# Attention: the combination's small sums on GpSimd over three turns, the last pair's quarters dealt to GpSimd and VectorE, the second branch stored in halves

## The chip, the cores and the metric

The kernel runs on one core of a Trainium2 chip. A core has five engines, each with its own queue of instructions that it works off in order: TensorE (PE in the profile) multiplies matrices and transposes, VectorE (DVE) and ScalarE (ACT) work on whole tiles, GpSimd (POOL) does elementwise work of the same kind, in this kernel on tiles outside TensorE's accumulators alone, and SyncE (SP) issues the transfers (DMAs) between the device's memory and the on-chip memory. Engines wait for one another by semaphores. The metric is device microseconds (us) of one launch, as the median of the runs.

## What is computed

One decoder layer over 2048 tokens of width 1024, all in float32. Half of the mixer's width is gated linear attention (GLA) in chunks, the other half is dilated attention with 8 heads of 64; then come an output projection, a squared-ReLU MLP and norms. The change lies in the dilated attention. Each head has three branches (window and dilation 128/1, 512/4 and 2048/16), and their results are weighted with a softmax over their log-sum-exps:

```python
def dilated_mixer(q, k, v, rel_bias):
    q = q * DSA_DH ** -0.5
    outs, lses = [], []
    for window, dilation in DSA_PATTERN:
        o, lse = dilated_branch(q, k, v, rel_bias, window, dilation)
        outs.append(o)
        lses.append(lse)
    w = jax.nn.softmax(jnp.stack(lses, axis=0), axis=0)
    return jnp.sum(w[..., None] * jnp.stack(outs, axis=0), axis=0)
```

The kernel doesn't form the log-sum-exps. For each token, head and branch it keeps the sum of the values weighted with exp(s - m), the sum of these weights (den) and nm = -m, the negated largest logit. The combination takes M, the smallest nm of the three branches, E = exp(M - nm), Z = the sum of E times den, and the weights E / Z.

## The kernel before

The kernel runs in stages, one after the other: the input projections, then the attention (the dilated attention with the GLA steps strewn into it), then the output projection and the MLP. In the projections and the MLP TensorE multiplies without a break; the change touches the attention alone, which lies between about 562 and 920 us.

**Units.** The dilated attention goes over four pairs of heads. A head has a sequence of 20 units: 4 for branch 2 (dilation 16), 8 for branch 1 (dilation 4), 8 for branch 0. So a pair has 40 units and the whole 160. In the last pair (pair 3) branches 2 and 1 of both heads come first and the branch-0 units of the two heads take turns of two at the end. The loop (L973) runs over units; in each turn three units at different stages are woven together instruction by instruction (`alternate`): the scores of the unit three ahead, the transposes of the present one and the values of the one two back.

- Scores: TensorE multiplies queries and keys into accumulator banks `ps_c` (L649 and L651); VectorE adds the bias and takes the minimum in one custom instruction (L661, tiles `pe` and `O`, where `O` takes nm), ScalarE forms the exponential (L662).
- Transposes: TensorE turns the weights into `ps_d` (L671); the copy into `pt` goes to ScalarE (L678) and to VectorE (L680) in turn.
- Values: TensorE multiplies `pt` with the values `v` into `ps_a` (L690); VectorE copies each finished group of four token blocks into `O` (L693).

So for every unit TensorE depends on VectorE at three places: L661 (its bank `ps_c` is free only when VectorE has read it), L680 and L693.

**The rest of the attention's work.** GLA steps follow one another at a fixed rate of 56 for each 100 units, using accumulator bank `ps_o` (L810 the decay, L823, L824, L867) and GpSimd for their elementwise work (L813, L816, L818, L860, L861, and the power in L98); VectorE adds the new state from `ps_o` (L870). GpSimd also packs each head's queries for branches 1 and 2 by casts (`pack_q`, L603, four pieces of 512 columns) and sets ones into the values' tile (L557). `load_v` (L554) fetches a pair's values; for branch 1 in four batches, one a unit.

**The combination.** The results of branches 2 and 1 stand in another order of tokens than those of branch 0. So when both heads of a branch are done, `store_branch` (L699) writes `O` out to `boD` and `combine_load` (L709) reads it back in token order into the tile `cmb`, half of the tokens (8 blocks of 128) at a time. `combine` (L717) then handles a half: 14 small sums on tiles of 128x16 (two minima L725 and L726, three subtractions L728, the denominators L730, L732, L733 twice, the reciprocal L734, three weights L736), and one Exp on ScalarE (L729). All 14 are on VectorE. Then come, for each four blocks, three 128x512 products (L742) and two additions (L744), on GpSimd. It is a generator that stops after the small sums and after each addition; `combine_at` (L927) gives it its turns. In pairs 0 to 2 the combination of a pair runs in the first units of the next pair, each half with 6 turns, the first three units after the pair's start. In pair 3 it runs in quarters of four blocks (sums of 128x8), at units that lie 8, 11, 14 and 18 after its branch-0 units begin, since the output projection's first tiles wait for it: TensorE's transposes of the first 8 token blocks take the last pair straight from `O` (L1051 and following). Quarter 12's products are on VectorE, those of the other three on GpSimd. The scratch `small` (128 x 96) is shared by both halves.

**What sets the order.** Each engine's queue is in the order that a tile scheduler makes of the program: it follows the program, and may put an instruction whose data it takes for ready ahead of others on the same engine. `keep_in_program_order` pins an instruction behind the one that was written before it on its engine. `issue_later` (L753) holds a transfer back for a number of units, `at_unit` plans a function for a unit.

Of the kernel before, what the change touches and what calls it, by code (L numbers as in the profile page):

```python
# [20 lines left out]
HT = NT // 2  # L21
# [19 lines left out]
def emit(tc, a, stop=99):  # L41
# [657 lines left out]
    def store_branch(pr, br, O):  # L699
        dst = boD[pr][br - 1]  # L700
        if br == 1:
            issue_later(3, dst.rearrange("(b p r) n -> p b (r n)", b=4, r=4),
                        O.rearrange("p (b r) n -> p b (r n)", b=4))
        else:
            issue_later(3, dst.rearrange("(p r) n -> p (r n)", r=16), O.rearrange("p r n -> p (r n)"))
# [11 lines left out]
    def combine(pr, t0, n, loaded, X):  # L717
# [3 lines left out]
        at = small[:, t0 // 4 % 2 * 48:] if n == 4 else small  # L721
# [3 lines left out]
        V.tensor_tensor(M, nm[0], nm[1], op=OP.min)  # L725
        V.tensor_tensor(M, M, nm[2], op=OP.min)  # L726
        for b in range(3):
            V.tensor_tensor(E[:, b], M, nm[b], op=OP.subtract)  # L728
        A.activation(E, E, AF.Exp)  # L729
        V.tensor_tensor(Z[:, 0], E[:, 0], den[0], op=OP.mult)  # L730
        for b in (1, 2):
            V.tensor_tensor(Z[:, 1], E[:, b], den[b], op=OP.mult)  # L732
            V.tensor_tensor(Z[:, 0], Z[:, 0], Z[:, 1], op=OP.add)  # L733
        V.reciprocal(Z[:, 1], Z[:, 0])  # L734
        for b in range(3):
            V.tensor_tensor(E[:, b], E[:, b], Z[:, 1], op=OP.mult)  # L736
# [28 lines left out]
    def gla_start():  # L765
# [16 lines left out]
        gst["sq"] = ub[:, 1800:1928]  # L782
        gst["gq"] = [view(uc[:, 256 * i:], (2, 128)) for i in range(2)]
# [128 lines left out]
    def after(b):  # L912
        pr, hh = divmod(b.h, 2)
        if hh and b.br:
            store_branch(pr, b.br, b.O)
        if hh and pr < 3:
            vs[pr + 1, b.br] = load_v(pr + 1, b.br, lambda n, *f: at_unit(clock[0] + AHEAD + 1 + n, *f))
# [9 lines left out]
    def combine_at(pr, t0, n, at, steps):  # L927
# [4 lines left out]
        def step():  # L932
            if (pr, t0) not in running:
                running[pr, t0] = combine(pr, t0, n, got[pr, t0 // 8], V if (pr, t0) == (3, 12) else G)
            next(running[pr, t0], None)
# [4 lines left out]
    for pr in range(4):  # L940
# [3 lines left out]
        for hh, br in seq:  # L944
# [7 lines left out]
            if br == 2 and first:  # L952
# [3 lines left out]
                if hh == 0:  # L956
                    for half in range(2):
                        combine_at(pr - 1, 8 * half, 8, first - 2 + 7 * half, [first + 3 + 7 * half + n for n in range(6)])
# [14 lines left out]
    for k in range(-AHEAD, NU + LAG):  # L973
# [18 lines left out]
        if 0 <= k - LAG:  # L992
            u = units[k - LAG]
            if u.ns[-1] == NT - 1:
                after(u.b)
    for _ in gla:
        pass
# [425 lines left out]
```

## Time and profile before

| | |
|---|---|
| median of 3 runs | 2352.82 us (2348.53 to 2355.7) |
| the profiled execution | 2354.68 us, with a span of 2352.9 us |
| TensorE busy, share of the span | 2292.8 us, 97% |
| VectorE | 1583.5 us, 67% |
| ScalarE | 1147.5 us, 49% |
| GpSimd | 467.3 us, 20% |
| mean granted TensorE clock | 0.992 |

A row of the timeline gives the start in us, the duration, the engine, the line, the operation, the tiles (out<-in), their shape, the number of instructions in the row, and in brackets the idle time of the engine ahead of it with what ended it. A row of the waits names the engine, the tile and line that waited, after the arrow what released it, then the sum of the waits in us, how many there were and the longest. A row of a group gives the number of instructions, the busy time and the mean duration in ns. A row of the windows gives a stretch, its length, each engine's busy time with its instructions, the granted TensorE clock (1.00 is full), the share of the DMA engines that were busy, and GB/s.

### The profile page before, as it was taken

How to read it: one execution, taken by the hardware profiler on the slowest of the kernel's cores; microseconds unless marked ns; L12 is line 12 of the kernel's file. 1: busy time of each engine (PE TensorE's matmuls, PEld its weight loads, DVE VectorE, ACT ScalarE, POOL GpSimd, SP SyncE). 2: the span in 40 equal slices, each digit the busy share in tenths (PEclk: the TensorE clock that was granted, in tenths of full speed). 3: DMA queues.
4: the chain of work that ended last, by engine and by line, in shares of the span. 5: the costliest groups of instructions: out<-in, count | busy, mean ns of one | idle time of the engine just before them, and what ended most of it. 6: DMA issues, size and time to landing. Idle time of an engine off the chain costs nothing.

```text
span 2352.9 us, 34987 instructions
## 1 busy us (share of the span) xinstructions
PE 2292.8 (97%) x12652; PEld 1978.6 (84%) x12652; DVE 1583.5 (67%) x2989; ACT 1147.5 (49%) x2200; POOL 467.3 (20%) x467
## 2 busy tenths in 40 slices
PE   6999999999999998999999999999999999999998
PEld 6978898689999988888888888888888888888887
DVE  7888778756677677345877779777764456446545
ACT  5665436435676664323655557555553223224323
POOL 0333324245486465100000000000000100001002
PEclk8999999999999999999999999999999999999999
DMA  4458754857676755567744447444476487457653
GB/s 151 138 166 246 223 176 121 256 166 235 193 231 212 251 166 195 188 215 255 252 163 148 148 148 273 148 150 155 155 262 238 170 283 246 145 179 250 207 169 108
DMA packets 341741, 457.59 MB, mean 194 GB/s; under 512 B 18053, under 2 KB 214166, under 8 KB 336192
## 3 DMA queue, kind: packets, MB, share of 16 engines
q1 hardware_dynamic: 336814, 446.71, 58.4%
q10 hardware_dynamic: 4754, 8.66, 1.0%
q8 instruction: 99, 1.62, 0.3%
q14 instruction: 74, 0.61, 0.1%
HBM read 292.99 MB, written 167.02 MB: 196 GB/s over the span
## 4 chain that ended last, share of the span: by engine, by line
PE 50%; DVE 1%; ACT 0%; issue 0%; POOL 0%; POOLq 0%
PE ps_c L67 6%; PE ps_c L68 6%; PE ps_c L66 6%; PE ps_a L68 4%; PE ps_a L67 4%; PE ps_a L66 4%; PE ps_d L66 4%; PE ps_d L68 4%; PE ps_d L67 4%; PE ps_o L68 2%; PE ps_o L67 2%; PE ps_o L66 2%; DVE hb L352 0%; ACT scr L1248 0%; DVE sumd L1254 0%; ACT hb L351 0%
## 5 line engine op out<-in xcount | busy, mean ns | idle before, releaser
L1250 POOL TENSOR_TENSOR suma<-suma,gs 128x512 f32<-128x512 f32 x16 | 23.3, 1474 | 1143.1 <-ACT scr L1248 1143.0
L352 DVE TENSOR_TENSOR ca<-ra,ca 128x1024 fp32r<-128x1024 f32 x112 | 137.6, 1230 | 162.1 <-ACT ca L351 161.9
L351 ACT ACTIVATE ca<-ra 128x1024 fp32r<-128x1024 f32 x112 | 118.0, 1053 | 219.5 <-PE ps_c L68 175.8
L351 ACT ACTIVATE w1comb<-w1raw 128x512 fp32r<-128x512 f32 x224 | 140.1, 627 | 156.3 <-PE ps_c L68 54.2
L690 PE MATMUL ps_a<-v,pt 128*128 128x65 f32 x1200 | 181.3, 254 | 8.8 <-DVE pt L680 7.5
L662 ACT ACTIVATE pe<-pe,O 128x256 f32<-128x256 f32 (+1 forms) x384 | 155.7, 454 | 67.1 <-DVE O L661 62.0
L352 DVE TENSOR_TENSOR w1comb<-w1raw,w1comb 128x512 fp32r<-128x512 f32 x224 | 153.9, 689 | 49.9 <-ACT w1comb L351 49.8
L690 PEld LDWEIGHTS ps_a<-v,pt 128*128 128x128 f32 x1200 | 176.9, 196 | 12.4 <-DVE pt L680 9.2
L671 PE MATMUL ps_d<-ident,pe 128*128 128x128 f32 x600 | 159.9, 280 | 0.0
L661 DVE CUSTOM_DVE_ANT_0 pe<-ps_c,nb 128x256 f32<-128x256 f32 (+1 forms) x384 | 126.0, 360 | 38.7 <-PE ps_d L671 17.0
L206 ACT ACTIVATE wcomb<-wraw 128x512 fp32r<-128x512 f32 (+2 forms) x126 | 96.9, 774 | 88.6 <-PE ps_o L67 19.3
L351 ACT ACTIVATE cb<-rb 128x1024 fp32r<-128x1024 f32 x56 | 59.4, 1061 | 164.5 <-PE ps_o L67 110.5
L67 PE MATMUL ps_c<-hb,w1comb 128*128 128x512 f32 x336 | 130.8, 389 | 0.7 <-DVE w1comb L352 0.7
L68 PE MATMUL ps_c<-hb,w1comb 128*128 128x512 f32 x336 | 130.7, 389 | 0.0
L66 PE MATMUL ps_c<-hb,w1comb 128*128 128x512 f32 x336 | 130.7, 389 | 0.0
L66 PE MATMUL ps_c<-cb,ca 128*128 128x512 f32 x336 | 130.7, 389 | 0.0
L67 PE MATMUL ps_c<-cb,ca 128*128 128x512 f32 x336 | 130.7, 389 | 0.0
L68 PE MATMUL ps_c<-cb,ca 128*128 128x512 f32 x336 | 130.7, 389 | 0.0
L208 DVE TENSOR_TENSOR wcomb<-wraw,wcomb 128x512 fp32r<-128x512 f32 (+2 forms) x84 | 96.3, 1150 | 36.0 <-ACT wcomb L206 35.6
L671 PEld LDWEIGHTS ps_d<-ident,pe 128*128 128x128 f32 x600 | 110.7, 189 | 0.3
L352 DVE TENSOR_TENSOR cb<-rb,cb 128x1024 fp32r<-128x1024 f32 x56 | 68.1, 1221 | 61.8 <-ACT cb L351 61.8
L1116 ACT ACTIVATE acc<-acc 128x512 f32<-128x512 f32 x128 | 79.7, 631 | 49.2 <-DVE acc L1136 34.9
(365 smaller groups left out, 7200.7 us busy)
## 6 DMA issues: line engine op xcount, KB each, us to landing
ra<-actD SPq DMA_DIRECT2D x56, 1024.0 KB, 7.2
actD<-acc SPq DMA_DIRECT2D x192, 256.0 KB, 2.4
rb<-w_ff SPq DMA_DIRECT2D x72, 512.0 KB, 4.6
w1raw<-w_ff SPq DMA_DIRECT2D x32, 1024.0 KB, 7.8
k<-kD SPq DMA_DIRECT2D x16, 1024.0 KB, 8.1
rb<-hTD SPq DMA_DIRECT2D x13, 1024.0 KB, 6.2
wraw<-w_in SPq DMA_DIRECT2D x48, 256.0 KB, 3.6
boD<-O SPq DMA_DIRECT2D x8, 1056.0 KB, 5.6
```

The source lines that it names most:

```text
L66: T.matmul(out, sh, mh, start=first, stop=False)
L67: T.matmul(out, sl, mh, start=False, stop=False)
L68: T.matmul(out, sh, ml, start=False, stop=last)
L206: A.activation(hi, src, AF.Copy, scale=sc)
L208: V.tensor_tensor(lo, src, hi.bitcast(F32), op=OP.subtract)
L351: A.activation(hi, src, AF.Copy)
L352: V.tensor_tensor(lo, src, hi.bitcast(F32), op=OP.subtract)
L661: V.tensor_tensor_reduce(p, s, bias, scale=1.0, scalar=BIG, op0=OP.add, op1=OP.min, accum_out=nm)
L662: A.activation(p, p, AF.Exp, bias=nm, scale=-1.0)
L671: T.transpose(pb[:, i * 128:i * 128 + 128], src, ident)
L690: T.matmul(self.b.opsum[:, n % 4], self.pt[:, i * 128:i * 128 + 128], self.b.v[:, blk, cols], start=first, stop=last)
L1116: A.activation(v, v, AF.Relu)
```

## The change

1. In pairs 0 to 2, 11 of a half's 14 small sums go to GpSimd: the three subtractions, the five operations for the denominators and the three weights. The two minima and the reciprocal stay on VectorE. The first minimum, the Exp and the reciprocal are pinned to the program's order. Two more stops in the generator spread the small sums over three turns (minima and subtractions; Exp and denominators; reciprocal and weights), and a half has 8 turns instead of 6, the first one unit later.
2. The second half has a scratch of its own (`gst["small"]`, in the tile that the profile calls `gla`).
3. In pair 3 the quarters that begin at block 0 and 8 are done by GpSimd, the small sums (without the minima and the reciprocal) and the products, and those that begin at block 4 and 12 by VectorE.
4. The store of branch 1 goes out in two halves, the first when the odd head's first eight blocks are done.
5. The four batches of the next pair's values lie two units apart, not one.

The lines move: of the changed kernel, L727 and L728 are the minima, L730 subtracts, L733 is the Exp, L734, L736 and L737 form the denominators, L740 is the reciprocal, L742 the weights, L748 the products and L750 the additions.

```diff
@@ -696,11 +696,12 @@
     class Branch:
         pass
 
-    def store_branch(pr, br, O):
+    def store_branch(pr, br, O, half=1):
         dst = boD[pr][br - 1]
         if br == 1:
-            issue_later(3, dst.rearrange("(b p r) n -> p b (r n)", b=4, r=4),
-                        O.rearrange("p (b r) n -> p b (r n)", b=4))
+            bs = slice(2 * half, 2 * half + 2)
+            issue_later(2 - half, dst.rearrange("(b p r) n -> p b (r n)", b=4, r=4)[:, bs],
+                        O.rearrange("p (b r) n -> p b (r n)", b=4)[:, bs])
         else:
             issue_later(3, dst.rearrange("(p r) n -> p (r n)", r=16), O.rearrange("p r n -> p (r n)"))
 
@@ -718,22 +719,27 @@
 
         ts = slice(t0, t0 + n)
         R = [outs[pr, 0][:, ts], *[r[:, t0 % 8:t0 % 8 + n] for r in loaded]]
-        at = small[:, t0 // 4 % 2 * 48:] if n == 4 else small
+        at = (small if t0 < 8 else gst["small"])[:, t0 // 4 % 2 * 48 if n == 4 else 0:]
         E, Z, M = view(at, (3, n, 2)), view(at[:, 6 * n:], (2, n, 2)), view(at[:, 10 * n:], (n, 2))
         nm = [r[:, :, 130:132] for r in R]
         den = [r[:, :, 0:130:129] for r in R]
-        V.tensor_tensor(M, nm[0], nm[1], op=OP.min)
+        W = X if pr == 3 else G
+        tc.keep_in_program_order(V.tensor_tensor(M, nm[0], nm[1], op=OP.min))
         V.tensor_tensor(M, M, nm[2], op=OP.min)
         for b in range(3):
-            V.tensor_tensor(E[:, b], M, nm[b], op=OP.subtract)
-        A.activation(E, E, AF.Exp)
-        V.tensor_tensor(Z[:, 0], E[:, 0], den[0], op=OP.mult)
+            W.tensor_tensor(E[:, b], M, nm[b], op=OP.subtract)
+        if pr < 3:
+            yield
+        tc.keep_in_program_order(A.activation(E, E, AF.Exp))
+        W.tensor_tensor(Z[:, 0], E[:, 0], den[0], op=OP.mult)
         for b in (1, 2):
-            V.tensor_tensor(Z[:, 1], E[:, b], den[b], op=OP.mult)
-            V.tensor_tensor(Z[:, 0], Z[:, 0], Z[:, 1], op=OP.add)
-        V.reciprocal(Z[:, 1], Z[:, 0])
+            W.tensor_tensor(Z[:, 1], E[:, b], den[b], op=OP.mult)
+            W.tensor_tensor(Z[:, 0], Z[:, 0], Z[:, 1], op=OP.add)
+        if pr < 3:
+            yield
+        tc.keep_in_program_order(V.reciprocal(Z[:, 1], Z[:, 0]))
         for b in range(3):
-            V.tensor_tensor(E[:, b], E[:, b], Z[:, 1], op=OP.mult)
+            W.tensor_tensor(E[:, b], E[:, b], Z[:, 1], op=OP.mult)
         yield
         for t in range(0, n, 4):
             rs = [r[:, t:t + 4, 1:129].rearrange("p t (h e) -> p t h e", h=2) for r in R]
@@ -780,6 +786,7 @@
         gst["kn"] = view(ub[:, 1032:], (2, 128))
         gst["g"] = [ub[:, 1288 + 256 * i:1544 + 256 * i] for i in range(2)]
         gst["sq"] = ub[:, 1800:1928]
+        gst["small"] = ub[:, 1928:2024]
         gst["gq"] = [view(uc[:, 256 * i:], (2, 128)) for i in range(2)]
         gst["gk"] = [view(uc[:, 512 + 256 * i:], (2, 128)) for i in range(2)]
         gst["gv"] = [uc[:, 1024 + 512 * i:1536 + 512 * i] for i in range(2)]
@@ -914,7 +921,7 @@
         if hh and b.br:
             store_branch(pr, b.br, b.O)
         if hh and pr < 3:
-            vs[pr + 1, b.br] = load_v(pr + 1, b.br, lambda n, *f: at_unit(clock[0] + AHEAD + 1 + n, *f))
+            vs[pr + 1, b.br] = load_v(pr + 1, b.br, lambda n, *f: at_unit(clock[0] + AHEAD + 1 + 2 * n, *f))
 
     units = []
     plan = {}
@@ -931,7 +938,7 @@
 
         def step():
             if (pr, t0) not in running:
-                running[pr, t0] = combine(pr, t0, n, got[pr, t0 // 8], V if (pr, t0) == (3, 12) else G)
+                running[pr, t0] = combine(pr, t0, n, got[pr, t0 // 8], V if pr == 3 and t0 % 8 else G)
             next(running[pr, t0], None)
 
         for k in steps:
@@ -955,7 +962,7 @@
                     at_unit(first - n, lambda p: next(p), pieces)
                 if hh == 0:
                     for half in range(2):
-                        combine_at(pr - 1, 8 * half, 8, first - 2 + 7 * half, [first + 3 + 7 * half + n for n in range(6)])
+                        combine_at(pr - 1, 8 * half, 8, first - 2 + 7 * half, [first + 4 + 7 * half + n for n in range(8)])
             if (pr, br) != (3, 0):
                 for n in range(0, NT, m):
                     units.append(Unit(b, range(n, n + m)))
@@ -993,6 +1000,8 @@
             u = units[k - LAG]
             if u.ns[-1] == NT - 1:
                 after(u.b)
+            elif u.ns[-1] == HT - 1 and u.b.h % 2 and u.b.br == 1:
+                store_branch(u.b.h // 2, 1, u.b.O, 0)
     for _ in gla:
         pass
     for k in range(NU + LAG + AHEAD, max(plan) + 1):
```

How the order of the engines' queues changes is shown at three places. The first is VectorE in the first units of pair 2, where the first half of pair 1 is combined (`O_6725`; `O_7541` is pair 2's). Before, nearly all the sums stand in a row between L661 steps:

```order
L725 TENSOR_TENSOR small<-O_6725,cmb 128x16
L661 ISA pe,O_7541<-ps_c,nb_5239 128x128
L661 ISA O_7541 128x1
L726 TENSOR_TENSOR small<-small,cmb 128x16
L661 ISA pe,O_7541<-ps_c,nb_5239 128x128
L661 ISA O_7541 128x1
L728 TENSOR_TENSOR small<-small,O_6725 128x16
L728 TENSOR_TENSOR small<-small,cmb 128x16 x2
L693 COPY O_6725<-ps_a 128x4x65
L680 COPY pt<-ps_d 128x512
L730 TENSOR_TENSOR small<-small,O_6725 128x16
L732 TENSOR_TENSOR small<-small,cmb 128x16
```

The same engine and combination in the changed kernel (`O_6721` is pair 1's, `O_7690` and `O_7539` are pair 2's), from the second minimum to the reciprocal:

```order
L728 TENSOR_TENSOR small<-small,cmb 128x16
L661 ISA pe,O_7690<-ps_c,nb_5266 128x256
L661 ISA O_7690 128x1
L693 COPY O_7539<-ps_a 128x4x65
L661 ISA pe,O_7690<-ps_c,nb_5266 128x256
L661 ISA O_7690 128x1
L680 COPY pt<-ps_d 128x256
L661 ISA pe,O_7690<-ps_c,nb_5266 128x256
L661 ISA O_7690 128x1
L693 COPY O_7539<-ps_a 128x4x65
L740 RECIPROCAL small<-small 128x16
L693 COPY O_7690<-ps_a 128x4x65
```

The subtractions, denominators and weights are gone from VectorE; three L661 steps, two copies of `O` and one of `pt` stand between the last minimum and the reciprocal.

The second place is GpSimd for the same half. Before, it has the products and additions, between the steps of the GLA:

```order
L97 TENSOR_SCALAR stats<-gla 128x4
L860 TENSOR_TENSOR gla<-gla 128x512
L98 TENSOR_TENSOR stats<-stats,mhalf 128x4
L742 TENSOR_TENSOR O_6725<-O_6725,small 128x4x128 x2
L742 TENSOR_TENSOR cmb<-cmb,small 128x4x128 x3
L861 TENSOR_TENSOR gla<-gla,stats 128x512
L742 TENSOR_TENSOR cmb<-cmb,small 128x4x128
L557 MEMSET v 128x16x2
L744 TENSOR_TENSOR O_6725<-O_6725,cmb 128x4x128 x2
```

In the changed kernel, on GpSimd (L820, L823 and L825 are the GLA's decay):

```order
L823 TENSOR_TENSOR gla<-gla 64x2x128 x2
L825 TENSOR_TENSOR gla<-gla 128x2
L820 TENSOR_TENSOR gla<-gla 128x256
L730 TENSOR_TENSOR small<-small,O_6721 128x16
L730 TENSOR_TENSOR small<-small,cmb 128x16 x2
L734 TENSOR_TENSOR small<-small,O_6721 128x16
L736 TENSOR_TENSOR small<-small,cmb 128x16
L737 TENSOR_TENSOR small<-small 128x16
L736 TENSOR_TENSOR small<-small,cmb 128x16
L737 TENSOR_TENSOR small<-small 128x16
L742 TENSOR_TENSOR small<-small 128x16 x3
L748 TENSOR_TENSOR O_6721<-O_6721,small 128x4x128 x2
```

The 11 sums stand in one block behind a decay of the GLA and ahead of the half's products.

The third place is VectorE in the last pair, at the end of the attention (`O_9505`, in the changed kernel `O_9507`, is pair 3's branch 0; L884 and L891 split the output projection's weights). Before:

```order
L734 RECIPROCAL small<-small 128x8
L884 TENSOR_TENSOR wo<-woraw,wo 128x1024
L732 TENSOR_TENSOR small<-small,cmb 128x8
L736 TENSOR_TENSOR small<-small 128x8 x3
L733 TENSOR_TENSOR small<-small 128x8
L734 RECIPROCAL small<-small 128x8
L736 TENSOR_TENSOR small<-small 128x8 x3
L693 COPY O_9505<-ps_a 128x4x65
L680 COPY pt<-ps_d 128x512
```

In the changed kernel, at the reciprocals of quarters 0 and 4:

```order
L740 RECIPROCAL small<-small 128x8 x2
L742 TENSOR_TENSOR small<-small 128x8
L891 TENSOR_TENSOR wo<-woraw,wo 128x1024
L742 TENSOR_TENSOR small<-small 128x8 x2
L748 TENSOR_TENSOR O_9507<-O_9507,small 128x4x128
L693 COPY O_9507<-ps_a 128x4x65
L680 COPY pt<-ps_d 128x512
L661 ISA pe,O_9507<-ps_c,nb_5301 128x256
L661 ISA O_9507 128x1
L748 TENSOR_TENSOR cmb<-cmb,small 128x4x128 x2
L891 TENSOR_TENSOR wo<-woraw,wo 128x1024
L680 COPY pt<-ps_d 128x512
```

Quarter 4's products now stand on VectorE between the copies and the L661 steps for which TensorE waits; one quarter's weights (L742) have left it.

## Prediction

> **What bounds the kernel now.** I read the page's first part, then a table of windows over the attention, then TensorE's list of waits there, and last the timeline around each long wait. The page's first part gives busy time by engine:
>
> ```profile
> span 2352.9 us, 34987 instructions
> PE 2292.8 (97%) x12652; PEld 1978.6 (84%) x12652; DVE 1583.5 (67%) x2989; ACT 1147.5 (49%) x2200; POOL 467.3 (20%) x467
> ```
>
> TensorE (PE) is busy for 97% of the span, so only its idle time and its clock can be won. The change touches the attention alone, so the next view is the windows of that stage: up to 630 us no combination runs, then come the stretches in which the combination of head pair 0, 1 and 2 runs, and the last 20 us before the output projection. After the length stand the busy times of PE, PE's loads, VectorE (DVE), ScalarE (ACT) and GpSimd (POOL), then the granted clock.
>
> ```profile
> 562.00:630.00 68.00, 68.00 (x628) 67.43 (x627) 47.17 (x198) 49.64 (x138) 35.87 (x49) 1.00 0.68 223
> 630.00:715.00 85.00, 82.47 (x732) 80.73 (x731) 62.88 (x275) 58.09 (x161) 58.85 (x67) 1.00 0.67 212
> 715.00:803.00 88.00, 85.92 (x752) 84.39 (x752) 62.89 (x275) 60.21 (x174) 61.00 (x71) 0.96 0.71 222
> 803.00:900.00 97.00, 89.35 (x759) 86.44 (x759) 73.24 (x300) 64.09 (x173) 50.74 (x57) 0.96 0.69 218
> 900.00:920.00 20.00, 15.17 (x117) 13.37 (x116) 17.73 (x52) 8.94 (x27) 17.75 (x17) 1.00 0.62 218
> ```
>
> Without a combination PE has no idle time at all; with one it loses 2.53, 2.08 and 7.65 us, and 4.83 us in the last stretch. Two stretches also have a clock under 1. So the combination is what stops PE. TensorE's list of waits in the attention says on whom:
>
> ```profile
> PE ps_a L690 <- DVE pt L680: 7.5, 8, 2.7
> PE ps_o L810 <- issue: 3.6, 2, 2.1
> PE ps_c L649 <- DVE O L661: 3.4, 3, 2.1
> PE ps_a L690 <- DVE O L693: 1.1, 1, 1.1
> PE ps_a L66 <- DVE O L693: 0.9, 1, 0.9
> PE ps_o L867 <- DVE gla L824: 0.3, 1, 0.3
> PE ps_a L690 <- ACT pt L678: 0.2, 1, 0.2
> ```
>
> Nearly all of it is VectorE, late with a copy or with the bias-and-minimum step (L661). GpSimd is in no row. The row "issue" names no one; the timeline shows what VectorE did then. Here are the long waits of PE with what VectorE and GpSimd did ahead of them (start, duration, instruction; in brackets the wait before it):
>
> ```profile
> 654.02 2.52 POOL L744 TENSOR_TENSOR O<-O,cmb 128x512 f32<-128x512 f32 x2
> 654.69 1.89 DVE L728 TENSOR_TENSOR small<-small,cmb 128x16 f32<-128x16 f32 x2
> 656.97 0.66 PE L690 MATMUL ps_a<-v,pt 128*128 128x65 f32 x4 [1.13 <-DVE O L693]
> ...
> 661.76 1.93 DVE L736 TENSOR_TENSOR small<-small 128x16 f32<-128x16 f32 x3
> 664.51 0.36 PE L649 MATMUL ps_c<-k,qs 128*128 128x256 f32 x1 [0.68 <-DVE O L661]
> ...
> 742.26 2.54 POOL L744 TENSOR_TENSOR O<-O,cmb 128x512 f32<-128x512 f32 x2
> 742.27 1.33 DVE L732 TENSOR_TENSOR small<-small,cmb 128x16 f32<-128x16 f32 x1
> 743.64 1.19 DVE L733 TENSOR_TENSOR small<-small 128x16 f32<-128x16 f32 x1
> 747.00 0.58 PE L649 MATMUL ps_c<-k,qs 128*128 128x256 f32 x1 [2.08 <-DVE O L661]
> ...
> 814.06 0.18 DVE L725 TENSOR_TENSOR small<-O,cmb 128x16 f32<-128x16 f32 x1 [4.60 <-DMA cmb<-boD]
> 815.10 0.57 PE L810 MATMUL ps_o<-gla 128*128 128x130 f32 x3 [1.56 <-issue]
> ...
> 833.45 1.25 DVE L728 TENSOR_TENSOR small<-small,cmb 128x16 f32<-128x16 f32 x1
> 834.62 3.86 POOL L603 CAST qp<-qs 128x512 fp32r<-128x512 f32 x4
> 835.44 0.39 PE L649 MATMUL ps_c<-k,qp 128*128 128x256 f32 x1 [0.62 <-DVE O L661]
> 836.55 0.90 DVE L732 TENSOR_TENSOR small<-small,cmb 128x16 f32<-128x16 f32 x1
> 838.32 0.90 PE L810 MATMUL ps_o<-gla 128*128 128x130 f32 x4 [2.08 <-issue]
> 839.88 0.69 PE L690 MATMUL ps_a<-v,pt 128*128 128x65 f32 x2 [0.66 <-DVE pt L680]
> ```
>
> A 128x16 sum is tiny, and a pair of them still holds VectorE for 1.9 us when GpSimd works on a product or a cast at the same time. At 814 VectorE stood for 4.60 us before a minimum whose data was still on its way.
>
> **Step 1: the waits that go.** In pairs 0 to 2, 11 of the 14 small sums of a half leave VectorE: the subtractions (L728), the weighted denominators (L730 to L733) and the weights (L736). Those are what stands ahead of the waits at 656.97, 664.51, 747.00, 835.44, 838.32 and 839.88. The two minima and the reciprocal stay, with a turn between each. The wait at 815.10 lies behind a minimum that a scheduler had pulled ahead of its data; after the change the minima are pinned to the program's place, a unit later (in the windows a pair of 40 units takes 88 us, so a unit is 2.2 us), and the store that feeds them goes out in two halves, the first one earlier. Removed: 1.13 + 0.68 + 2.08 + 1.56 + 0.62 + 2.08 + 0.66 = 8.8 us.
>
> **Step 2: the clock.** The two stretches under full clock come right behind the two waits of 2.08 us; a third row is the stretch behind the longest wait, in the last pair:
>
> ```profile
> 746.50:753.30 6.80, 6.30 (x27) 5.92 (x28) 4.82 (x20) 4.35 (x12) 6.63 (x8) 0.50 0.75 197
> 838.60:845.50 6.90, 6.24 (x34) 5.94 (x33) 4.31 (x24) 4.23 (x14) 4.92 (x6) 0.51 0.19 59
> 905.00:908.00 3.00, 2.99 (x27) 2.94 (x28) 3.00 (x7) 1.47 (x5) 3.00 (x3) 1.00 0.97 341
> ```
>
> The timeline has that longest wait:
>
> ```profile
> 902.35 1.67 DVE L736 TENSOR_TENSOR small<-small 128x8 f32<-128x8 f32 x3
> 905.01 0.44 PE L690 MATMUL ps_a<-v,pt 128*128 128x65 f32 x2 [2.68 <-DVE pt L680]
> ```
>
> At half clock PE needs twice the time, so 6.30/2 + 6.24/2 = 6.3 us are lost there. I take it that the waits cause them and that they go too: 8.8 + 6.3 = 15.1 us. Against it speaks the third row: after 2.68 us of waiting the clock stayed at 1.00. The Trainium skill, "TensorE: Matmul & The Clock Gate" (section "HAM oscillation — how this bites in real kernels"), puts the limit at idle gaps over some 3.4 us; by it none of these waits would halve the clock and step 2 would bring nothing, 8.8 instead of 15.1. The trace shows half clock after 2.08 us twice, so I side with the trace, and keep the other as a rival.
>
> **Step 3: what the sums cost on GpSimd.** The trace has no such sum there; the nearest rows are a small two-input product on GpSimd, and VectorE's own weights with their spread (minimum, median and maximum in ns):
>
> ```profile
> L818 POOL TENSOR_TENSOR gla<-gla 128x2 f32<-128x2 f32 x15 | 3.0, 198 | 1.0
> L736 DVE TENSOR_TENSOR small<-small x30: 151/168/1005, 641.1 to 922.6; 128x16 f32<-128x16 f32 x18, 128x8 f32<-128x8 f32 x12
> L742 DVE TENSOR_TENSOR cmb<-cmb,small x2: 1526/1659/1792, 924.0 to 925.4; 128x512 f32<-128x512 f32 x2
> L742 DVE TENSOR_TENSOR O<-O,small x1: 803/803/803, 923.3 to 923.3; 128x512 f32<-128x512 f32 x1
> ```
>
> At 0.2 us, 11 sums take 2.2 us of a half; at the worst VectorE price of 1.0 us, 11. GpSimd is busy for 58.85 of 85 and 61.00 of 88 us, so two halves (4.4 to 22 us) fit, and PE waits for GpSimd in no row. I take 0.2 us and no cost on PE's path. If that cover were gone, it would show as VectorE waiting for GpSimd, the slower rival below. Nothing below zero can come of it, since GpSimd only gets work.
>
> **Step 4: the new waits in pairs 0 to 2.** The reciprocal on VectorE must now wait for GpSimd's denominators, and those for ScalarE's Exp. In the changed order four L661 steps or more stand between Exp and reciprocal in five of the six halves; in pair 1's first half both fall behind the same L661 step. There VectorE waits for the Exp and five sums of 0.2 us, about 2 us, and behind the reciprocal in its queue stand the O copy (L693) and the next L661, for which PE waits. The nearest row is VectorE held for 1.89 us at 654.69, which cost PE 1.13: I take 1.2, with 0 and 2.68 (905.01) as ends. In pair 2's first half the pinned Exp follows right behind the minimum, so ScalarE waits for three subtractions on GpSimd, with the transposes' copies (L678) and the next Exp (L662) queued behind: between 0 and the 1.13 of that row, 0.6.
>
> **Step 5: the last pair.** VectorE loses the sums of quarters 0 and 8, 22 of 56 (11 each), and gains quarter 4's three products and two additions. Beside an idle GpSimd that is 3 × 0.80 plus two more at no more than that, 4.0 at most, less 22 × 0.168 = 3.7: +0.3. Beside a busy GpSimd the products cost 1.66 us, five of them 8.3, and the removed sums cost more as well: the three of 902.35 took 1.67, 0.56 each, which as an upper price gives 12.3. So the ends are -4.0 (8.3 less 12.3) and +4.6 (8.3 less 3.7). GpSimd is busy 17.75 of the 20 us, which speaks for the dear products, while the removed sums lie between 0.168 and 0.56; at 0.31 each they are 6.8, and 8.3 - 6.8 = 1.5 us is what I take. The Trainium skill, "SBUF — State Buffer" (section "Who interferes with whom"), has a VectorE instruction with two inputs in that memory shut out a GpSimd one that reads it, and the other way round, for the whole instruction; that is a rule against dealing quarters to both engines at once, and by it the term would stand at its upper end, 4.6. The trace agrees as far as 0.80 and 1.66 go. The halved stores add four transfers to issue, and the next pair's values are only fetched further apart: nothing on PE's list waits for either, 0.
>
> **The sum.** 15.1 - 1.2 - 0.6 - 1.5 = 11.8 us less. The profiled execution took 2354.68 us and stood 1.86 above the median of its runs, 2352.82; I set the sum against the median, since that is what is measured: 2341.0 us. About 0.3%, 7.06 us, can be told from no change, so "faster" is below 2345.8.
>
> **The rivals.**
>
> More is won. The new waits cost nothing and the last stretch loses its idle time as well, since the sums at 902.35 leave VectorE: 15.1 + 4.83 = 19.9, 2332.9 us. For it: the 2.68 us wait of PE lies right behind them. Against it: quarter 4's products come to the same engine at the same time.
>
> The clock does not come back. The half-clock stretches have another cause or move: 8.8 - 3.3 = 5.5, 2347.3 us, no change. For it: 905.01, above. Against it: both stretches lie at a 2.08 us wait, and no third one is there.
>
> The last pair jams. VectorE's quarter 4 and GpSimd's quarter 0 hold each other up; the term stands at 4.6, and one half-clock stretch of 3.15 us follows: 15.1 - 1.8 - 7.75 = 5.55, 2347.3 us. For it: 0.80 against 1.66 us. Against it: both engines also lose work there.
>
> Slower: the wait moves from GpSimd to VectorE. The sums stand in GpSimd's one queue behind casts and products; four casts alone take 3.86 us (834.62), and with five sums of 0.2 us a chain is 4.9 us long, more than a turn of 2.2. If the reciprocal then holds VectorE for the difference, 2.7 us, PE loses the 2.08 us of 838.32 and half a stretch of 6.30: 5.2 us each time. Six halves give 31.2 + 2.1 - 15.1 = +18.2, 2371.0 us. Costs and gains meet at 13.0/5.2 = 2.5 halves, and four are over the bound (+7.8, 2360.6 us). For it: in pairs 0 and 1 GpSimd is as busy as ScalarE, in few long pieces. Against it: Exp and reciprocal stand apart in five of six halves.
>
> **How the numbers follow.** My forecast has 0.54; more is won 0.06; the clock 0.12; the jam 0.13; slower 0.15. So faster 0.60, no change 0.25, slower 0.15. The range begins at the best case, 2333, and ends with the two rivals near 2347.3 plus the open ends of steps 4 and 5 (1.5, 0.5 and 3.1 us), 2353; it leaves out the slower rival and little else.
>
> **What would show it.** Right (the lines are those of the changed kernel, where L730 subtracts, L734 to L737 form the denominators, L740 is the reciprocal and L742 the weights): 128x16 sums on GpSimd at about 0.2 us; PE idle for 2.53 - 1.81 = 0.7 us in pair 0, 2.08 - 2.08 + 1.2 = 1.2 in pair 1, 7.65 - 4.92 + 0.6 = 3.3 in pair 2's stretch; a clock of 1.00 through the attention; one wait of VectorE of about 2 us for GpSimd, at pair 1's first reciprocal. Wrong: waits of VectorE at L740 in most halves, GpSimd sums near 1 us, half-clock stretches that stay without a long wait, or an idle time over 6 us in the last 20 us.

## The result and the profile after

The changed kernel takes 2338.53 us (median of 5 runs, 2336.11 to 2342.39), the kernel before 2352.82 (2348.53 to 2358.35): a ratio of 0.9938, with a 95% interval of 0.9919 to 0.9958. So it is faster by 14.3 us, where 11.8 were forecast. The profiled execution has a span of 2334.3 us, 18.6 less than before; it was the fastest of its five (2336.11) and the one before stood 1.86 above its median, which is 4.3 of the 18.6. The page's first part:

```profile
span 2334.3 us, 35003 instructions
PE 2285.9 (98%) x12652; PEld 1975.0 (85%) x12652; DVE 1572.9 (67%) x2906; ACT 1146.8 (49%) x2200; POOL 484.1 (21%) x550
```

GpSimd has 83 instructions and 17 us more, VectorE 83 fewer. The windows of the changed kernel's attention (columns as before: stretch, length, busy times, granted clock, transfers):

```profile
630.00:715.00 85.00, 85.00 (x763) 84.03 (x763) 59.13 (x256) 60.90 (x176) 60.72 (x90) 1.00 0.63 203
715.00:803.00 88.00, 88.00 (x794) 87.08 (x794) 61.92 (x264) 61.81 (x179) 64.11 (x91) 1.00 0.78 246
803.00:865.00 62.00, 62.00 (x551) 61.02 (x550) 48.15 (x193) 44.97 (x124) 47.93 (x69) 1.00 0.71 222
865.00:905.00 40.00, 33.82 (x262) 31.30 (x261) 34.71 (x92) 24.55 (x64) 37.37 (x55) 0.91 0.77 241
```

While the combinations of pairs 0 to 2 run, TensorE no longer stops in this execution and keeps its full clock; all that is lost lies in the last pair, 6.18 us of idle time and a clock of 0.91. TensorE's list of waits in the attention and the first tiles of the output projection says the same:

```profile
PE ps_d L671 <- ACT pt L678: 3.3, 1, 3.3
PE ps_o L860 <- ACT gla L852: 2.0, 2, 1.0
PE ps_a L690 <- DVE pt L680: 0.5, 1, 0.5
PE ps_a L690 <- ACT pt L678: 0.3, 1, 0.3
```

VectorE is nearly gone from it, where it had been in almost every row. In its place stands ScalarE. The sums on GpSimd, from the view of the tile `small` (minimum, median and maximum in ns):

```profile
L742 POOL TENSOR_TENSOR small<-small x12: 197/220/225, 654.5 to 886.6; 128x16 f32<-128x16 f32 x9, 128x8 f32<-128x8 f32 x3
```

They take 0.22 us, and hardly vary. Of all 88 sums on GpSimd 87 take between 0.20 and 0.26 us; one takes 1.14 (at 838.97 us, beside a split of the weights on VectorE, L891, of 1.23). The timeline around the one long wait that is left:

```profile
886.78 2.11 DVE L891 TENSOR_TENSOR wo<-woraw,wo 128x1024 fp32r<-128x1024 f32 x1 [0.27 <-ACT wo L890]
...
887.77 3.03 POOL L748 TENSOR_TENSOR cmb<-cmb,small 128x512 f32<-128x512 f32 x2
...
889.51 1.06 ACT L890 ACTIVATE wo<-woraw 128x1024 fp32r<-128x1024 f32 x1 [1.88 <-DMA woraw<-w_out]
889.82 1.53 DVE L748 TENSOR_TENSOR O<-O,small 128x512 f32<-128x512 f32 x1
...
890.76 0.58 ACT L678 ACTIVATE pt<-ps_d 128x512 f32<-128x512 f32 x1
...
891.39 1.11 PE L671 MATMUL ps_d<-ident,pe 128*128 128x128 f32 x4 [3.27 <-ACT pt L678]
```

ScalarE stood for 1.88 us ahead of a piece of the projection's weights whose transfer was late, with the copy for TensorE (L678) behind it in its queue; beside it, GpSimd's products for quarter 0 and VectorE's for quarter 4 ran at 1.5 us each.

**Where the 18.6 us came from.** The windows before:

```profile
565.00:865.00 300.00, 289.62 (x2541) 284.06 (x2540) 215.00 (x928) 203.04 (x570) 195.14 (x227) 0.98 0.65 207
865.00:945.00 80.00, 73.30 (x536) 66.34 (x535) 62.67 (x183) 42.18 (x111) 37.73 (x40) 1.00 0.66 217
```

PE's idle time (a window's length less PE's busy time) fell from 10.38 + 6.70 us there to 0.00 + 6.18 in the same two windows of the changed kernel: 10.9 us. Half-clock stretches lost 6.3 us before, and now 4.11 / 2 = 2.1 (one stretch from 888.7 us): 4.2 us. The first value product came at 561.33 us instead of 562.68: 1.4 us, ahead of anything that the change touches. The other 2.1 us I can't place.

### The profile page after: what moved, and what is told of

The parts are those of the page before. It is cut to its first block, busy times and chain, and to the rows that moved or that the text cites. A ratio compares the mean times of both kernels' runs of the same rounds, so it can differ in the third digit from the quotient of the medians.

```text
span 2334.3 us, 35003 instructions
## 1 busy us (share of the span) xinstructions
PE 2285.9 (98%) x12652; PEld 1975.0 (85%) x12652; DVE 1572.9 (67%) x2906; ACT 1146.8 (49%) x2200; POOL 484.1 (21%) x550
## 4 chain that ended last, share of the span: by engine, by line
PE 84%; DVE 6%; DMA 3%; issue 3%; ACT 2%; POOL 1%; POOLq 0%; DVEq 0%; SPq 0%; ACTq 0%
PE ps_a L67 8%; PE ps_a L68 8%; PE ps_a L66 8%; PE ps_c L66 7%; PE ps_c L67 7%; PE ps_c L68 7%; PE ps_a L690 4%; PE ps_d L66 4%; PE ps_d L68 4%; PE ps_d L67 4%; PE ps_o L66 3%; PE ps_o L67 3%; PE ps_o L68 3%; PE ps_d L671 3%; PE ps_c L649 2%
## 5 line engine op out<-in xcount | busy, mean ns | idle before, releaser
L352 DVE TENSOR_TENSOR ca<-ra,ca 128x1024 fp32r<-128x1024 f32 x112 | 137.8, 1231 | 166.7 <-ACT ca L351 166.7
L352 DVE TENSOR_TENSOR w1comb<-w1raw,w1comb 128x512 fp32r<-128x512 f32 x224 | 154.0, 689 | 50.6 <-ACT w1comb L351 50.5
L661 DVE CUSTOM_DVE_ANT_0 pe<-ps_c,nb 128x256 f32<-128x256 f32 (+1 forms) x384 | 125.7, 361 | 35.2 <-PE ps_d L671 14.8
L352 DVE TENSOR_TENSOR cb<-rb,cb 128x1024 fp32r<-128x1024 f32 x56 | 68.3, 1222 | 59.6 <-ACT cb L351 59.4
L98 POOL TENSOR_TENSOR stats<-stats,mhalf 128x1 f32<-128x1 f32 (+1 forms) x64 | 47.8, 752 | 273.7 <-DVE stats L97 273.7
```

The lines of the kernel that those rows point to most:

```text
L98: G.tensor_tensor(r2, r, mhalf[:, :n], op=OP.pow)
L352: V.tensor_tensor(lo, src, hi.bitcast(F32), op=OP.subtract)
L661: V.tensor_tensor_reduce(p, s, bias, scale=1.0, scalar=BIG, op0=OP.add, op1=OP.min, accum_out=nm)
```

## The experiments

The theories. Theory 1: VectorE's small sums, slow beside GpSimd's work, and its waits ahead of the minima held up its queue and with it TensorE; taking the sums off VectorE wins. Theory 2: the new order (turns, pins, later start) wins, on whichever engine. Theory 3: the last pair's deal wins. Two things of the change are in force in the last pair as well wherever an edit leaves them in: the pins, and the second scratch for quarters 8 and 12. No run takes them out of the last pair alone. The table has every run; the idle time is PE's, in the windows 565 to 865 us (pairs 0 to 2, in nearly all of it) and 865 to 945 us (the last pair and the first tiles of the projection), with the granted clock of the latter. Idle time and clock are those of one profiled execution, which lay within 4.2 us of the run's median (stores_loads_only: 7.5 below it), so differences of an idle time of 1 or 2 us say little: the control after_again has the same code as the changed kernel.

| run | median us | ratio to before, 95% interval | idle to 865 | idle from 865 | clock from 865 |
|---|---|---|---|---|---|
| before | 2352.8 | | 10.4 | 6.7 | 1.00 |
| changed kernel | 2338.5 | 0.9938 (0.9919 to 0.9958) | 0.0 | 6.2 | 0.96 |
| after_again | 2337.5 | 0.9938 (0.9923 to 0.9952) | 1.5 | 6.9 | 0.96 |
| sums_on_vector | 2342.1 | 0.9964 (0.9951 to 0.9978) | 5.6 | 3.7 | 0.96 |
| last_pair_old | 2338.4 | 0.9943 (0.9931 to 0.9956) | 1.0 | 5.1 | 0.91 |
| engine_only | 2334.6 | 0.9929 (0.9916 to 0.9941) | 1.7 | 2.1 | 0.98 |
| last_pair_only | 2352.4 | 0.9999 (0.9986 to 1.0011) | 9.5 | 5.6 | 0.96 |
| order_only | 2338.3 | 0.9940 (0.9923 to 0.9957) | 6.0 | 2.9 | 1.00 |
| stores_loads_only | 2351.0 | 0.9994 (0.9983 to 1.0005) | 11.7 | 2.5 | 1.00 |
| one_turn | 2351.1 | 0.9997 (0.9987 to 1.0006) | 2.5 | 11.9 | 0.87 |
| no_products | 2345.2 | 0.9975 (0.9965 to 0.9985) | 5.6 | 4.9 | 0.94 |
| sums_thrice | 2349.0 | 0.9984 (0.9975 to 0.9994) | 1.0 | 11.5 | 0.89 |
| after_wo34 | 2345.7 | 0.9978 (0.9969 to 0.9987) | 2.0 | 10.7 | 0.89 |
| eng_wo34 | 2346.6 | 0.9977 (0.9968 to 0.9986) | 2.0 | 9.9 | 0.89 |

**The engine alone.** In the kernel before, `W = V if pr == 3 else G` for the 11 sums, nothing else:

```diff
-            V.tensor_tensor(E[:, b], M, nm[b], op=OP.subtract)
+            W.tensor_tensor(E[:, b], M, nm[b], op=OP.subtract)
```

> The kernel before, with only the engine of the 11 small sums of a half in pairs 0 to 2 changed from VectorE to GpSimd: no turns more, no pins, one shared scratch, stores, loads and the last pair as before. Theory 1: 7.3 us of waits and 6.3 us of half clock go, 2340 to 2345 us. Theory 2: no gain, about 2353, or slower, since VectorE waits for GpSimd at the reciprocal without turns between. Theory 3: about 2353.

2334.6 us, the fastest of all, and below what theory 1 had allowed. TensorE's waits in the attention, and VectorE's that concern the combination:

```profile
PE ps_a L690 <- DVE pt L680: 3.1, 5, 1.4
PE ps_o L824 <- POOL gla L814: 0.6, 1, 0.6
```

```profile
DVE small L726 <- DMA cmb<-boD: 7.1, 7, 3.6
DVE small L727 <- DMA cmb<-boD: 2.0, 2, 1.2
DVE small L735 <- POOL small L734: 1.3, 1, 1.3
```

In the kernel before, VectorE's waits ahead of the minima were these:

```profile
DVE small L725 <- DMA cmb<-boD: 12.9, 6, 4.6
DVE small L726 <- DMA cmb<-boD: 3.1, 4, 1.9
```

As theory 1 has it: of the 10.4 us of idle time in pairs 0 to 2, 8.7 are gone, although VectorE still waits 9.1 us for its data ahead of the minima (L726, L727; 16.0 before). I read this so that those waits now find VectorE with nothing queued that TensorE would miss for long. VectorE waits for GpSimd at one reciprocal only. What goes beyond theory 1 lies in the last pair, which this edit doesn't touch: 2.1 us of idle time there instead of 6.7.

**The order alone, and the sums back on VectorE.** The first has turns, pins, second scratch and later start in the kernel before; the second is the changed kernel with

```diff
-        W = X if pr == 3 else G
+        W = X if pr == 3 else V
```

> The kernel before with the combination's new order in pairs 0 to 2 alone: turns, pins, second scratch and the start one unit later; all small sums on VectorE, the last pair, the store and the loads as before. Theory 1a (two costs: VectorE's 16 us of waits for the cmb transfers ahead of its minima, and sums that are slow beside GpSimd; taking either away frees enough of VectorE): 2341 to 2346 us, the waits for cmb near 0. Theory 1b (only the slow sums count; what won with the sums on VectorE came from the earlier stores): 2350 to 2354 us.

> The changed kernel, but in pairs 0 to 2 all small sums stay on VectorE; turns, pins, scratch, stores and the last pair as changed. Theory 1 (VectorE's sums are slow beside GpSimd and hold up its queue, so moving them off wins): most of the waits come back, 1.13 + 0.68 + 2.08 + 0.62 + 2.08 + 0.66 = 7.3 us and perhaps half-clock stretches of 3.1 us each: 2346 to 2352 us. Theory 2 (the later, pinned and spread order wins, on whichever engine): within 2 us of the changed kernel's 2338.5. Theory 3 (the last pair's deal wins): also about 2338.5.

2338.3 and 2342.1 us: the order by itself gains more than theory 1 allowed, in either of its forms, and the second run lies between the two theories. In the order alone VectorE no longer waits for the `cmb` transfers at all (16.0 us before). The sums themselves are no faster: of the 84 on tiles of 128x16, 20 take over 0.5 us, and they sum to 32.5 us (17 and 28.4 before). So TensorE's waits behind VectorE are still there, at the same kind of place; the two longest rows:

```profile
PE ps_a L690 <- DVE pt L680: 5.1, 4, 2.1
PE ps_c L649 <- DVE O L661: 1.9, 1, 1.9
```

By the table the order takes 4.4 us of idle time to 865 us, the engine move 8.7. The order's total is as good as the whole change's because half-clock stretches cost only 3.40 / 2 = 1.7 us (one, from 750 us) instead of 6.3, and because the last pair lost 2.9 us instead of 6.7; its deal is as before, but the pins and the second scratch are in force there. The two cures overlap: the whole change is no faster than either.

**Stores and loads alone.** The branch-1 store in two halves, the values' batches two units apart:

> The kernel before with the store of branch 1 in two halves and the next pair's values two units apart, nothing else. Theory 1a: the transfers come somewhat earlier, VectorE's 16 us of waits for cmb shrink by less than half, 2348 to 2353 us. Theory 1b: 2340 to 2345 us.

2351.0 us, no change. VectorE's waits ahead of the minima barely shrink, from 16.0 to 13.9 us, while with the new order they are gone; so it is the later, pinned minima that do away with them (the two weren't taken apart):

```profile
DVE small L726 <- DMA cmb<-boD: 10.7, 5, 7.1
DVE small L727 <- DMA cmb<-boD: 3.2, 5, 1.0
```

**The last pair alone, and all but the last pair.**

```diff
-        W = X if pr == 3 else G
+        W = V if pr == 3 else G
...
-                running[pr, t0] = combine(pr, t0, n, got[pr, t0 // 8], V if pr == 3 and t0 % 8 else G)
+                running[pr, t0] = combine(pr, t0, n, got[pr, t0 // 8], V if (pr, t0) == (3, 12) else G)
```

> The kernel before, with only the last pair's quarters dealt as in the change (0 and 8 on GpSimd, 4 and 12 on VectorE, small sums and products). Theory 1 and 2: 2351 to 2355 us, no change that can be measured. Theory 3: 2340 to 2345 us.

> The changed kernel, but the last pair as before: all small sums of its quarters on VectorE, quarter 12's products on VectorE, those of the other three on GpSimd. Theory 1: 2337 to 2341 us, since the deal itself was priced at +1.5 us. Theory 2: the same. Theory 3 (the last pair's deal wins): most of the 14.3 us is lost again, 2348 us or more, with PE's waits of 1.2 to 2.7 us back in the last 20 us of the attention.

2352.4 and 2338.4 us: the deal is worth nothing either way, and theory 3 falls. Undoing it swaps the wait near 890 us: instead of 3.3 us for ScalarE's copy, TensorE waits 3.5 for VectorE's, which is behind small sums of 0.90 to 1.19 us beside GpSimd's products and additions, and behind a split of the weights:

```profile
886.04 2.07 POOL L748 TENSOR_TENSOR cmb<-cmb,small 128x512 f32<-128x512 f32 x2
886.23 0.90 DVE L737 TENSOR_TENSOR small<-small 128x8 f32<-128x8 f32 x1
...
888.08 1.27 POOL L750 TENSOR_TENSOR O<-O,cmb 128x512 f32<-128x512 f32 x1
888.17 1.19 DVE L737 TENSOR_TENSOR small<-small 128x8 f32<-128x8 f32 x1
...
889.52 1.21 DVE L891 TENSOR_TENSOR wo<-woraw,wo 128x1024 fp32r<-128x1024 f32 x1
```

**Without GpSimd's products and additions.** In the kernel before, for pairs 0 to 2:

```diff
-                X.tensor_tensor(r, r, wb, op=OP.mult)
+                if pr == 3:
+                    X.tensor_tensor(r, r, wb, op=OP.mult)
```

> The kernel before without GpSimd's 128x512 products and additions of pairs 0 to 2 (15 per half): that part of the output isn't computed; the small sums stay on VectorE and the order's program is the same. If VectorE's sums are slow because GpSimd works beside them, those with over 0.5 us fall from 17 to 5 or fewer (casts and GLA steps are still there) and their sum from 28.4 us to 16 to 20 for 84; PE's idle time ahead of 865 us falls from 10.4 to about 5, where the waits for cmb remain. If their length has another cause, both stay.

The idle time to 865 us fell to 5.6 as expected; but VectorE's waits for `cmb` fell with it, from 16.0 to 11.2 us, so that not all of this is due to the sums. The sums became shorter, but by less than expected: 23.6 us for 84 instead of 28.4. The group that lost most, between 562 and 865 us, first in the kernel before, then without the products (after the count: busy time, mean ns):

```profile
L733 DVE TENSOR_TENSOR small<-small 128x16 f32<-128x16 f32 x12 | 5.7, 475 | 0.3
```

```profile
L733 DVE TENSOR_TENSOR small<-small 128x16 f32<-128x16 f32 x12 | 3.5, 296 | 0.1
```

A mean of 475 became 296 ns, and not the 176 ns that half of these instructions took before. Of the 17 sums over 0.5 us 9 are left, where 5 had been expected. At 176 ns each the 84 would take 14.8 us; 13.6 us were above that before, and 8.8 are left. So GpSimd's products and additions make some of VectorE's sums slow, and about two thirds of the excess has another source. The timelines name it. Before, each of the 17 ran beside a GpSimd instruction for nearly its whole length: 8 beside an addition (L744), 5 beside a cast (L603), 4 beside a GLA step (L813, L860). Of the 9 that are left, 7 run beside a cast and 2 beside a GLA step, as here:

```profile
744.10 1.44 POOL L818 TENSOR_TENSOR gla<-gla 64x256 f32<-64x256 f32 x2 [1.22 <-ACT gla L813]
744.32 0.50 DVE L730 TENSOR_TENSOR small<-small,O 128x16 f32<-128x16 f32 x1
...
745.80 1.08 POOL L603 CAST qp<-qs 128x512 fp32r<-128x512 f32 x1
745.83 0.92 DVE L733 TENSOR_TENSOR small<-small 128x16 f32<-128x16 f32 x1
```

Sums with no GpSimd instruction beside them for more than a tenth of their length (reciprocals aside) never took over 0.19 us: 28 of them before, 46 here.

**More sums on GpSimd.** Three subtractions and three products, each three times:

```diff
-            W.tensor_tensor(E[:, b], M, nm[b], op=OP.subtract)
+            for _ in range(3 if pr < 3 else 1):
+                W.tensor_tensor(E[:, b], M, nm[b], op=OP.subtract)
```

> The changed kernel with eight more pairs of small sums: the three subtractions and the three products of the denominators run three times over on GpSimd in pairs 0 to 2 (12 instructions more of 0.22 us, 2.6 us a half, same results). Theory 1 (GpSimd's queue has room, the sums cost PE nothing): 2336 to 2341 us as the changed kernel, PE's idle time ahead of 865 us under 2 us. The slower rival (VectorE waits at the reciprocal as soon as GpSimd is later): 2.6 us more of waiting in each of six halves, 2345 us or more.

The point in dispute came out as theory 1 has it: idle to 865 us 1.0, and VectorE waits at no reciprocal for a `small` sum. But the time is 2349.0, which the rival had forecast for another reason, and the loss is in the last pair, which this edit does not touch: 5.3 us more of idle time than in the changed kernel, and a clock of 0.89. There the queues have another order:

```profile
904.68 0.52 POOL L745 TENSOR_TENSOR small<-small 128x8 f32<-128x8 f32 x3 [1.11 <-DVE small L743]
...
906.33 2.49 POOL L751 TENSOR_TENSOR cmb<-cmb,small 128x512 f32<-128x512 f32 x2
...
907.84 2.14 DVE L751 TENSOR_TENSOR cmb<-cmb,gla 128x512 f32<-128x512 f32 x2
909.90 2.53 DVE L753 TENSOR_TENSOR O<-O,cmb 128x512 f32<-128x512 f32 x2
...
912.46 0.37 SPq L770 DMA_DIRECT2D mixD<-O  x1
...
917.19 1.12 PE L377 MATMUL ps_c<-ident,mx 128*128 128x128 f32 x4 [6.14 <-DMA mx<-mixD]
```

GpSimd gets the reciprocal of quarter 0 at 904 us (at 886.01 in the changed kernel), its products meet VectorE's of quarter 12, whose store leaves at 912.46, and TensorE waits 6.14 us for the reload.

**One turn.** The changed kernel without the two stops:

```diff
-        if pr < 3:
-            yield
```

> The changed kernel without the two additional stops, so that a half's small sums stand in one turn again (on GpSimd, pins kept). If the spread over turns keeps VectorE from waiting for GpSimd at the reciprocal (the slower rival of the prediction), VectorE now waits about 2 us in each of six halves and PE loses 1 to 2 us each time: 2344 to 2350 us. If the order of the queues does that without the turns, no change, 2335 to 2340 us.

2351.1 us, a little above the first case's range, and not for its reason: VectorE's waits for GpSimd at reciprocals come to 1.3 us in the whole attention, and idle to 865 us is 2.5. Most of the loss is again in the last pair, 11.9 us of idle time and a clock of 0.87. There VectorE works on the small sums of quarter 12 beside GpSimd's products and additions:

```profile
905.23 1.20 DVE L728 TENSOR_TENSOR gla<-gla,cmb 128x8 f32<-128x8 f32 x1
...
907.35 2.09 DVE L730 TENSOR_TENSOR gla<-gla,cmb 128x8 f32<-128x8 f32 x2
907.36 2.05 POOL L744 TENSOR_TENSOR cmb<-cmb,gla 128x512 f32<-128x512 f32 x2
...
915.20 0.68 DVE L352 TENSOR_TENSOR mT<-ps_d,mT 128x512 fp32r<-128x512 f32 x1
...
915.93 0.90 PE L377 MATMUL ps_d<-ident,mx 128*128 128x128 f32 x3 [6.20 <-DVE mT L352]
```

Between 905 and 915 us eight of these sums take 0.95 to 1.30 us each (in the changed kernel two of quarter 12's are as slow). Behind them in VectorE's queue stands the step that empties a bank of the output projection's transposes (L352), for which TensorE waits 6.20 us; ScalarE stands 6.5 us at the pinned Exp, until the subtractions are done. It is theory 1's mechanism, in the last pair.

**The weights earlier.** To do away with the wait at 891 us, in the changed kernel and in the fastest one:

```diff
-        at_unit(NU - 28 + 3 * i + AHEAD, load_wo, 1)
+        at_unit(NU - 34 + 3 * i + AHEAD, load_wo, 1)
```

> The changed kernel with the eight pieces of the output projection's weights loaded and split six units earlier. If the wait of 3.3 to 4.2 us near 890 us comes from these splits in the queues of ScalarE and VectorE beside the last pair's quarters, it goes together with the half-clock stretch: 3.3 + 2.1 us less, about 2333 us. If it comes from the quarters alone, no change, 2336 to 2340 us.

> The kernel before with the engine of the small sums alone changed (as in the run engine_only), and the output projection's weights six units earlier. Its idle time behind 865 us was 2.1 us and its half-clock loss 1.7: at most that is to be won, 2331 to 2335 us.

2345.7 and 2346.6 us, slower by 7 and 12 instead of faster. In the changed kernel with the weights earlier:

```profile
865.09 1.65 DVE L891 TENSOR_TENSOR wo<-woraw,wo 128x1024 fp32r<-128x1024 f32 x1 [1.74 <-ACT wo L890]
865.61 5.02 POOL L748 TENSOR_TENSOR cmb<-cmb,small 128x512 f32<-128x512 f32 x4
...
869.78 1.93 DVE L891 TENSOR_TENSOR wo<-woraw,wo 128x1024 fp32r<-128x1024 f32 x1 [2.71 <-ACT wo L890]
...
872.32 0.58 PE L649 MATMUL ps_c<-k,qs 128*128 128x256 f32 x1 [6.29 <-DVE O L661]
```

The wait of 3.3 us near 890 is gone; one of 0.93 until 895.47 is left. But another of 2.70 comes until 909.18, and the pieces now meet pair 2's products: VectorE stands for 2.71 us ahead of a split (L891), with the L661 for which TensorE waits queued behind it. The splits do stop TensorE, so far the idea held; moving them only moved the stop, and made it longer.

**A control.** The changed kernel once more:

> The changed kernel once more, as a control beside the other three: about 2338.5 us, PE's waits in the attention about 6 us.

2337.5 us, with 8.4 us of idle time: the place near 890 us is the same, its length differs (4.2 instead of 3.3 us), and 1.5 us are lost in pair 1, where the first execution lost nothing.

**What stays open.** In the runs that took 2345.7 us or more, two are the old combination with 9.5 and 11.7 us of idle time in pairs 0 to 2, and four have almost none there and 9.9 to 11.9 us in the last pair, where the others have 2.1 to 6.9. So the last pair decides between the versions that cure pairs 0 to 2, and edits far ahead of it change it. Their longest waits differ, but in three of the four they stand behind quarter 12 on VectorE: behind its slow sums in one_turn, behind its products and additions in eng_wo34 (4.25 us, until 916.24), and behind its store in sums_thrice; in after_wo34 it is the splits. What puts quarter 12 there isn't settled. None of the kernels fixed the last pair's order by hand beyond the pins, and none took the pins out of it, which would have told. That engine_only is faster than the whole change isn't shown either: their intervals overlap.

## Why the prediction was right

The forecast of 2341.0 us, faster, came out at 2338.5. By its steps:

- **Step 1, the waits (8.8 us)**: right, and a little small. All 10.4 us of idle time to 865 us went, 8.9 in the control. The engine move by itself takes 8.7 of them. That a sum is long because GpSimd works beside it is shown; but the additions, casts and GLA steps count, not the products and casts alone that the prediction named.
- **Step 2, the clock (6.3 us)**: right for pairs 0 to 2; both stretches went with their waits. The clock of 1.00 through the attention that it forecast did not come. The Trainium skill, "TensorE: Matmul & The Clock Gate" (section "HAM oscillation — how this bites in real kernels"), names idle gaps over some 3.4 us; waits of 2.08 us had sufficed here. A new stretch in the last pair gave 2.1 back.
- **Step 3, the price on GpSimd**: 0.2 us forecast, 0.22 measured, at no cost for TensorE. Twelve sums more in a half cost it about nothing in pairs 0 to 2 either (1.0 us idle, 0.0 and 1.5 without them).
- **Step 4, the new waits (1.2 + 0.6)**: the waits came where they were expected. VectorE waited at pair 1's first reciprocal, and ScalarE for 0.2 us at an Exp:

```profile
DVE small L740 <- POOL small L737: 1.8, 1, 1.8
```

  TensorE lost nothing by it (0 us idle in the windows of pairs 0 and 1, where 0.7 and 1.2 had been expected to stay, and 0 from 803 to 865 us), so this term was too large by 1.8 us: these two waits did not become waits of TensorE. The 3.3 us expected for pair 2's stretch were for 803 to 900 us, and there 6.18 stayed, all behind 865 us, in the last pair.
- **Step 5, the last pair (+1.5)**: idle time 0.5 less, clock 2.1 more, together +1.6. The size fits by luck, for the reason given doesn't hold: the deal of the quarters changes nothing by itself (0.9999), and without it the rest of the change is as fast. The place doesn't fit either: the loss was looked for in the last 20 us of the attention, where TensorE now has no idle time (900 to 920 us), and it lies between 865 and 900. VectorE's products at 1.5 us beside GpSimd's are there as forecast, but with or without them something in that stretch stops TensorE.
- **The rivals.** Slower, by VectorE waiting for GpSimd in most halves, did not come true, even with twelve sums more. The jam of the last pair came true in part (3.27 us and one half-clock stretch), over ScalarE's queue.

The gain is 2.5 us more than forecast, about as much as the two profiled executions of the changed kernel differ by in idle time (6.2 and 8.4 us). What the prediction did not see: that the order without the engine move would have been as good, and that small shifts upstream move the last pair by some 10 us, idle time and half clock together.

## What to carry to other kernels

Small instructions in front of a critical queue are priced by what runs beside them: 0.17 us by the median, over 1 us beside GpSimd's long ones; look at the maximum of a group before calling it cheap. Where two cures (less work on the engine, or work placed when its data is there) remove the same stop, test each alone, since one may do. And when a scheduler orders the queues, compare versions by stretch: here 12 more sums in pairs 0 to 2 changed the idle time there by 1 us and that of the last pair by 5.3.

## What the runs showed of the hardware

The clock's halving doesn't go by one wait's length. In the run engine_only it followed a wait of 1.44 us; in last_pair_old it followed two of 1.04 and 0.34 us within 4 us; in the kernel before a wait of 2.68 us left it at 1.00. In order_only both happen in one execution: a wait of 2.08 us until 665.44 left the clock at 1.00, and one of 1.86 until 749.75 was followed by 0.51 from 750.00 to 753.40 us. Nor does it wait for the end of a stop: in the changed kernel the clock fell at about 888.7 us, 0.6 us into the wait of 3.27 and after one of 0.99. The first fence is the window of engine_only, the second that of last_pair_old:

```profile
888.10:891.50 3.40, 3.40 (x16) 3.02 (x16) 3.40 (x8) 0.92 (x2) 3.14 (x3) 0.51 0.12 48
```

```profile
867.50:874.30 6.80, 6.40 (x29) 5.72 (x28) 5.74 (x16) 4.89 (x12) 6.48 (x9) 0.50 0.76 198
```

These stretches are 3.4 and 6.8 us long, so that one wait of 1.44 us, or two of 1.04 and 0.34, cost another 3.40 / 2 = 1.7 and 6.40 / 2 = 3.2 us. What goes into the count besides the length is open.

The sums that vary from 0.15 to 1.3 us on VectorE took 0.20 to 0.26 us on GpSimd in 87 of 88 cases of the changed kernel. They aren't safe there either: one took 1.14 us beside a VectorE instruction of 1.23, and of the 160 in sums_thrice ten took over 0.5, eight of them in the last pair.
